# Opening token mixing with tokens standing and 512 columns of queries, keys and values moving, in a TensorE-bound two-layer trunk

## The chip, the cores and the metric

One core of one Trainium2 chip runs the whole program in one launch. The metric is device microseconds of one execution, from start to end; the time given for a kernel is the median of several runs. The engines in this text are TensorE (PE in the profile, PEld for its weight loads), VectorE (DVE), ScalarE (ACT), GpSimd (POOL) and SyncE (SP), which here only issues DMAs.

## The reference

Two layers (DEPTH 2) work on one sequence of 512 tokens by 1024 channels, in fp32. Each layer is a half-weighted SwiGLU block, a mixing block, and a second SwiGLU block:

```python
x = x + 0.5 * swiglu(rms_norm(x, ffn1_norm[l]), ffn1_wg[l], ffn1_wu[l], ffn1_wd[l])
h = rms_norm(x, mix_norm[l])
z = h @ w_in[l]                    # 1024 -> 2304 columns
q = z[..., :512]                   # 8 query heads of 64
k = z[..., 512:640]                # 2 key heads of 64
v = z[..., 640:768]                # 2 value heads of 64
attn_out = sliding_window_attention(q, k, v, attn_sink[l])
conv_out = short_conv(z[..., 768:1280], z[..., 1280:1792], z[..., 1792:], conv_w[l])
x = x + concatenate([attn_out, conv_out], -1) @ w_out[l]
x = x + 0.5 * swiglu(rms_norm(x, ffn2_norm[l]), ffn2_wg[l], ffn2_wu[l], ffn2_wd[l])
```

A last `rms_norm` follows the second layer. Attention works in blocks of 128 queries, each against its own and the previous block of 128 keys, with a bias that falls with the distance and a learned sink in the softmax. Four query heads share one key head.

## The kernel before

**Products.** TensorE's products need more precision than one fp32r product has, so each operand is split into a rounded part (hi) and the remainder (lo), and each product is three: hi x hi, hi x lo, lo x hi. ACT makes a weight's hi (line 222), DVE its lo (line 223). Raw weights come as tiles of 512 KB from HBM, most of them on SP's queue, in the order that `plan` writes down; `order` is the list of operand tiles, `need_split(g)` makes hi and lo up to tile g and issues the raw loads of some tiles further ahead (LOAD_AHEAD 4), `take_split` hands out the next tile. There are eight raw buffers and four each for hi and lo. The large products (SwiGLU, w_out) use a seven-product scheme of 2 x 2 blocks (class `Seven`), which needs sums of operand blocks.

**What stands and what moves.** A TensorE matmul has a 128 x 128 operand standing and another one moving past it. `group` (line 304) lets a tile of 128 weight columns stand and all 512 tokens move: 8 channel blocks x 3 = 24 matmuls give z for 128 columns, turned, with columns on the partitions and tokens along the row. `plain_halves`, which opens each SwiGLU block (from line 1097 on, its matmuls are the rows "up"), does it the other way: 128 tokens stand and 512 weight columns move; four weight tiles of 256 channels x 512 columns are held, and the products are done for the first 256 tokens, then for the second 256. Its result has tokens on the partitions. It is turned into columns on the partitions by a DMA: DVE and ACT write the fp32 numbers as two planes of 16 bits into a "room" (`apart`), two transposing DMAs on SP's queue turn each plane (`send`), and ACT joins the planes again (`join`).

**The norm and the opening of mixing.** The norm ahead of mixing is made in two halves of 256 tokens, because the second half's input is finished later. For each half, ACT sums squares (`Norm.__call__`), ACT makes a first guess of the reciprocal root (line 650), DVE mends it with one Newton step and scales the tokens to `xn` (line 661); `pull` then has TensorE turn xn (line 685), ACT copy hi and DVE the remainder. While the first half's turned norm is there and the second's is not, TensorE must have something to do: that is `halves` (lines 339 to 362). It holds three weight tiles (keys, values, first queries: MIX_COLS starts 2, 0 with two tiles of 128 columns each), and does for each the 24 products with 256 tokens moving, first for the first token half and then for the second; the second half's turns stand in between.

The results are `kacc`, `vacc` and `qacc`, each with its 128 columns on the partitions and 512 tokens along the row. Keys are copied straight from PSUM into kh and kl, each head at both partition halves (lines 1500 to 1506). Values are needed with tokens on the partitions: `take_values` copies vacc to SBUF and has TensorE turn it four times (line 1513). In the loop of lines 1663 to 1676 the first queries come from qacc and the other three from `group`; ACT writes hi scaled by 1/8 and DVE lo.

**Attention.** A unit is one block of 128 queries with one key head and its four query heads. `attend(step)` starts those stages of units that are due at that step by the lists at lines 44 to 49. `scores` does eight matmuls, DVE adds the bias and finds the maximum, ACT makes the exponentials (line 1565), DVE scales them by the sum (line 1573). `turn` has TensorE turn the probabilities (rows "pt", line 1623); for units whose entry in SEND_AT is a number it is done by 16-bit planes and transposing DMAs instead. `values` does the product with the values. The first scores stand at step 5, the first `turn` at step 6; step j + 2 follows the queries j, and the steps after that stand one behind each of the twelve products of the convolution's columns.

**Order.** The order on each engine is that of the program text, as far as a planner decides that an instruction is not ready; `issue_after` and `behind` pin an instruction behind another one, and `by_hand` to `by_itself` fix TensorE's order to the written one around the opening.

**Copies of the second SwiGLU block's norm.** Behind mixing stands another norm. Its `turn` also keeps a full-precision copy (`keep`, on ACT), which is put on the list `later` (lines 707 and 710) to be issued behind an instruction named by a string: "squared" is the last sum of squares on ACT, "added" a DVE addition of the block sums, "guess" the first guess of the root on ACT.

Of the kernel before, what the change touches and what calls it, by code (L numbers as in the profile page):

```python
# [8 lines left out]
F32 = mybir.dt.float32  # L9
# [7 lines left out]
P = 128  # L17
D = 1024
S = 512
# [57 lines left out]
def trunk_kernel(  # L77
# [32 lines left out]
    def psum(tag, shape, name):  # L110
        return ps.tile(shape, F32, tag=tag, bufs={"mm": 4, "sc": 2, "aux": 2}[tag], name=name)
# [215 lines left out]
    def by_itself():  # L327
        state["region"].__exit__(None, None, None)

    def hold(norm, n):  # L330

        first = state["group"]
        if norm.added:
            for ahead, one in ((2, norm.added), (3, norm.first)):
                with behind(one):
                    need_split(first + ahead)
        return [take_split(SPLIT_AHEAD - j)[1:] for j in range(n)]

    def halves(norm, n, done):

        first = state["group"]
        held = hold(norm, n)
        accs = [psum("mm", [P, S], f"acc_{first + j}") for j in range(n)]
        for t in range(2):
            for half in range(2):
                for j, (hi, lo) in enumerate(held):
                    for k in range(KC // 2 * half, KC // 2 * (half + 1)):
                        xh, xl = norm.half(k, t)
                        for i, (w, x_) in enumerate(((hi, xh), (hi, xl), (lo, xh))):
                            nc.tensor.matmul(  # L350
                                accs[j][:, t * H : (t + 1) * H],
                                w[:, k, :],
                                x_,
                                start=t + k + i == 0,
                                stop=k == KC - 1 and i == 2,
                                skip_group_check=True,
                            )
                    if not t and half and j < 2:
                        norm.pull()
                    if t and half:  # L360
                        need_split(first + j + SPLIT_AHEAD + 1)
                        done(j, accs[j])

    def down(acts, blocks, open_):

# [81 lines left out]
    def plan():  # L447
# [66 lines left out]
    MIX_COLS = (2, 0, 1, 5, 7, 3, 6, 8, 4)  # L514
    plan()


# [64 lines left out]
    class Norm:  # L582
# [39 lines left out]

        def __call__(self, t, o):

            self.squared = nc.scalar.activation(
                junk(f"sq_{self.i}_{t}_{o}"),
                xt(t, o),
                AF.Square,
                accum_out=self.ss[:, o * NT + t : o * NT + t + 1],
            )  # L630
# [48 lines left out]
        def turn(self, t, o, xn):  # L679

            name = f"{self.i}_{t}_{o}"
            tok = slice(t * P, (t + 1) * P)
            tp = psum(self.tags.pop(0), [P, KC // 2, P], f"xt_{name}")
            for j in range(KC // 2):
                nc.tensor.transpose(tp[:, j, :], xn[:, j * P : (j + 1) * P], ident)
# [12 lines left out]

            def keep():
                if not self.mixing:  # L700
                    nc.scalar.copy(self.full[o][:, :, tok], tp)

            if self.later is None:
                rest()
                keep()
            elif o:
                self.later.extend(((rest, "added"), (keep, "squared")))
            else:
                rest()
                self.later.append((keep, "squared"))  # L710

        def go_on(self):

# [293 lines left out]
    def ffn(norm, stages, whole, after=None, late=None):  # L1007
# [41 lines left out]
        def plain_halves(b):  # L1049
# [37 lines left out]
            for half in range(2):  # L1087
# [2 lines left out]
                ups = g2(f"up_{name}_{half}", F32, (P, 2, H))  # L1090
                for j, (wh, wl) in enumerate(held):
                    for t in range(2):
                        tok = slice(t * P, (t + 1) * P)
                        for k in range(2):
                            xh, xl = norm.half(2 * j + k, half)
                            for i, (x_, w) in enumerate(((xh, wh), (xl, wh), (xh, wl))):
                                nc.tensor.matmul(  # L1097
                                    accs[t],
                                    x_[:, tok],
                                    w[:, k, :],  # L1100
                                    start=j + k + i == 0,
                                    stop=j == 3 and k == 1 and i == 2,
                                )
                        if j == 3:
                            nc.scalar.activation(ups[:, t, :], accs[t][:, :H], AF.Silu)
                            nc.vector.tensor_mul(ups[:, t, :], accs[t][:, H:], ups[:, t, :])
# [380 lines left out]
    def mix(l, norm, after):  # L1487
# [8 lines left out]
        kacc, vacc, qacc = opened  # L1496
# [3 lines left out]
        for g in range(NKV):  # L1500
            own = slice(g * HD, (g + 1) * HD)
            other = slice((1 - g) * HD, (2 - g) * HD)
            nc.scalar.copy(kh[g][own, :], kacc[own, :])
            nc.vector.tensor_sub(kl[g][own, :], kacc[own, :], f32(kh[g][own, :]))
            nc.scalar.copy(kh[g][other, :], f32(kh[g][own, :]))
            nc.scalar.copy(kl[g][other, :], f32(kl[g][own, :]))

        def take_values():
            vf = g2(f"vf_{l}")
            nc.scalar.copy(vf, vacc)  # L1510
            vp = psum("aux", [P, NT, NKV, HD], f"vp_{l}")
            for t in range(NT):
                nc.tensor.transpose(
                    vp[:, t].rearrange("p g d -> p (g d)"), vf[:, t * P : (t + 1) * P], ident
                )


            vv = g8(f"vv_{l}", F32R, (P, NT * NKV, 2, HD))
            vsrc = vp.rearrange("p t g d -> p (t g) d")
            nc.scalar.copy(vv[:, :, 0, :], vsrc)  # L1520
            nc.vector.tensor_sub(vv[:, :, 1, :], vsrc, f32(vv[:, :, 0, :]))
            return vv

        class Unit:

# [134 lines left out]
                        done = getattr(unit, stages.get(at, "join"))() or done  # L1660
            return done

        for j in range(NH // 2):
            acc = group(norm.h) if j else qacc
            if j == 3:
                vv = take_values()
            if j % 2 == 0:
                room = both(f"q_{l}_{j}", shape=(P, 2, 2, S))
            qe, qo = room[j % 2][:, 0, :], room[j % 2][:, 1, :]
            for z, a, b in ((qe, slice(0, HD), slice(HD, P)), (qo, slice(HD, P), slice(0, HD))):  # L1670
                nc.scalar.activation(z[a, :], acc[a, :], AF.Copy, scale=1.0 / 8.0)
                nc.vector.scalar_tensor_tensor(
                    z[b, :], acc[a, :], 1.0 / 8.0, f32(z[a, :]), op0=ALU.mult, op1=ALU.subtract
                )
            q[2 * j], q[2 * j + 1] = qe, qo
            attend(2 + j)


        step = 6

# [87 lines left out]
```

## Time and profile before

| | |
|---|---|
| median of three runs | 1642.06 us (1641.43 to 1642.24) |
| the profiled execution | 1641.66 us, of which the span of the page is 1639.9 us |
| mean granted TensorE clock | 0.999 of full speed |
| instructions | 21080 |
| HBM read, written | 263.74 MB, 2.10 MB (162 GB/s over the span) |
| moved by hardware queue q1, by software queue q0 | 227.99 MB, 78.65 MB |
| chain that ended last, by engine | PE 92%, DVE 4%, ACT 1%, DMA 1% |

The profile is one execution. A busy time is the time in which an engine had at least one instruction under way; matmuls overlap each other, and their weight loads (PEld) run beside them. A row of the timeline reads: start in us from the start of the span, length in us, engine, line of the kernel, instruction, output <- inputs, tile shape, count; in brackets stands the idle time of the engine ahead of it and who ended that. In the lists of groups, the two numbers behind the bar are the busy time in us of all and the mean ns of one, then the idle time ahead of them. In the view of waits, a row says which engine's group waited, for whom, and then the total in us, how often, and the longest wait.

### The profile page before, as it was taken

What the parts mean: (1) busy time and instruction counts of PE and PEld (TensorE: products, weight loads), DVE (VectorE), ACT (ScalarE), POOL (GpSimd) and SP (SyncE); (2) the same over time, 40 slices, a digit from 0 to 9 for tenths busy, and PEclk for the clock granted to TensorE, in tenths of its full rate; (3) what the DMA queues carried; (4) which work ended last, traced back from release to release, by engine and by line L of the source; (5) the groups of instructions that cost most, each with busy time, mean ns of one, the idle gap of its engine ahead of it and who ended that gap; (6) DMA issues with size and microseconds to landing.
All of it is one profiled execution on the core that took longest, in us unless ns stands there. A gap on an engine that the chain in (4) does not pass through costs nothing.

```text
span 1639.9 us, 21080 instructions
## 1 busy us (share of the span) xinstructions
PE 1629.8 (99%) x7576; PEld 1356.7 (83%) x7576; DVE 1300.8 (79%) x1718; ACT 1128.7 (69%) x1581; POOL 193.5 (12%) x172
## 2 busy tenths in 40 slices
PE   9999999999999999999999999999999999999998
PEld 7888888888888888888888888888988888888886
DVE  7987779877799867798788677896578987768895
ACT  7457777556867667786576777865587775777864
POOL 0011111100111111112001111110002101111111
PEclk9999999999999999999999999999999999999999
DMA  9379999932685788999837898996137857999991
GB/s 257 86 196 219 225 215 256 221 93 58 167 205 129 205 205 206 218 228 248 231 78 204 207 218 220 232 250 194 53 90 167 208 131 191 213 224 223 227 263 65
DMA packets 286844, 308.64 MB, mean 188 GB/s; under 512 B 108532, under 2 KB 171028, under 8 KB 286740
## 3 DMA queue, kind: packets, MB, share of 16 engines
q1 hardware_dynamic: 244212, 227.99, 47.8%
q0 software_dynamic: 41824, 78.65, 28.1%
q8 instruction: 59, 0.97, 0.2%
q10 hardware_dynamic: 704, 0.66, 0.1%
q14 instruction: 45, 0.37, 0.1%
HBM read 263.74 MB, written 2.10 MB: 162 GB/s over the span
## 4 chain that ended last, share of the span: by engine, by line
PE 92%; DVE 4%; ACT 1%; DMA 1%; issue 1%; SPq 0%; ACTq 0%; DVEq 0%
PE x L941 25%; PE y L941 13%; PE x_s L941 10%; PE w L941 6%; PE y_s L941 5%; PE down L373 3%; PE acc L314 3%; PE acc L315 3%; PE acc L317 3%; PE up L1097 3%; PE w_s L941 3%; PE acc L350 2%; DVE wl L223 1%; PE acc L839 1%; DMA raw<-in_w_out_dram 1%
## 5 line engine op out<-in xcount | busy, mean ns | idle before, releaser
L223 DVE TENSOR_TENSOR wl<-raw,wh 128x1024 fp32r<-128x1024 f32 (+1 forms) x493 | 596.2, 1214 | 219.9 <-ACT wh L222 216.7
L222 ACT CAST wh<-raw 128x1024 fp32r<-128x1024 f32 (+1 forms) x493 | 513.2, 1046 | 312.2 <-PE y L941 41.6
L941 PE MATMUL y<-wh,ft 128*128 128x512 f32 x608 | 187.3, 389 | 0.0
L941 PE MATMUL x<-wh,fb 128*128 128x512 f32 x608 | 187.3, 389 | 0.0
L941 PE MATMUL x<-wh,ft 128*128 128x512 f32 x608 | 187.3, 389 | 0.0
L941 PEld LDWEIGHTS x<-wh,ft 128*128 128x128 f32 x608 | 114.1, 188 | 23.7
L941 PEld LDWEIGHTS x<-wh,fb 128*128 128x128 f32 x608 | 114.1, 188 | 23.7
L941 PEld LDWEIGHTS y<-wh,ft 128*128 128x128 f32 x608 | 114.1, 188 | 23.7
L941 PE MATMUL y<-wl,ft 128*128 128x512 f32 x304 | 118.3, 389 | 0.0
L941 PE MATMUL x<-wl,fb 128*128 128x512 f32 x304 | 118.3, 389 | 0.0
L941 PE MATMUL x<-wl,ft 128*128 128x512 f32 x304 | 118.3, 389 | 0.0
L217 POOL DMA_DIRECT2D raw<-in_ffn_wu_dram x39 | 47.3, 1222 | 544.3 <-DMA raw<-in_ffn_wu_dram 327.0
L1266 ACT COPY raw_a<-pt 128x1024 uint16<-128x1024 uint16 x76 | 103.2, 1358 | 11.1 <-DMA pt<-pl 11.1
L314 PE MATMUL acc<-hh,wh 128*128 128x512 f32 x240 | 94.7, 394 | 0.0
L315 PE MATMUL acc<-hl,wh 128*128 128x512 f32 x240 | 93.8, 391 | 0.0
L317 PE MATMUL acc<-hh,wl 128*128 128x512 f32 x240 | 93.7, 391 | 0.0
L941 PE MATMUL w<-wh,fb 128*128 128x512 f32 x304 | 93.6, 389 | 0.0
L941 PE MATMUL x_s<-wh,ft_s 128*128 128x512 f32 x256 | 78.8, 389 | 0.0
L941 PE MATMUL y_s<-wh,ft_s 128*128 128x512 f32 x256 | 78.8, 389 | 0.0
L250 DVE TENSOR_TENSOR raw<-raw,raw 128x1024 f32<-128x1024 f32 x58 | 70.6, 1222 | 7.1 <-DMA raw<-in_ffn_wd_dram 5.9
L217 POOL DMA_DIRECT2D raw<-in_ffn_wg_dram x39 | 47.1, 1212 | 233.7 <-DVE u L1250 62.3
L941 PE MATMUL x_s<-wh,fb_s 128*128 128x512 f32 x240 | 73.9, 389 | 0.0
(364 smaller groups left out, 3421.3 us busy)
## 6 DMA issues: line engine op xcount, KB each, us to landing
raw<-in_ffn_wu_dram SPq DMA_DIRECT2D x120, 512.0 KB, 5.2
raw<-in_ffn_wd_dram SPq DMA_DIRECT2D x104, 512.0 KB, 6.3
raw<-in_ffn_wg_dram SPq DMA_DIRECT2D x80, 512.0 KB, 4.9
raw<-in_ffn_wu_dram POOLq DMA_DIRECT2D x39, 512.0 KB, 8.1
raw<-in_ffn_wg_dram POOLq DMA_DIRECT2D x39, 512.0 KB, 6.0
raw<-in_w_in_dram SPq DMA_DIRECT2D x36, 512.0 KB, 4.3
raw<-in_ffn_wd_dram POOLq DMA_DIRECT2D x32, 512.0 KB, 8.5
raw<-raw POOLq DMA_DIRECT2D x20, 512.0 KB, 8.5
```

The costliest lines, as they stand in the source:

```text
L217: nc.gpsimd.dma_start(out=r, in_=rows_of(*more), accum_op=ALU.add)
L222: cast = nc.scalar.copy(hi, raw)
L223: state["sub"] = eng.tensor_sub(lo, raw, f32(hi))
L250: nc.vector.tensor_add(a11, a11, s1)
L314: nc.tensor.matmul(acc, hi[:, k, :], rhs[k][0], start=k == first, stop=False)
L315: nc.tensor.matmul(acc, hi[:, k, :], rhs[k][1], start=False, stop=False)
L317: nc.tensor.matmul(acc, lo[:, k, :], rhs[k][0], start=False, stop=k == last)
L350: nc.tensor.matmul(accs[j][:, t * H : (t + 1) * H], w[:, k, :], x_, start=t + k + i == 0, stop=k == KC - 1 and i == 2, skip_group_check=True,)
L373: nc.tensor.matmul(acc, a[:, k, tok], w[:, k, :], start=i + k + n == 0 and fresh[t], stop=i == last and k == 1 and n == 2, skip_group_chec ...
L941: nc.tensor.matmul(accs[u], x_[:, 2 * h + k, tok], w[:, k, :], start=start and h + k + i == 0, stop=h + k == 2 and i == 2, skip_group_chec ...
L1097: nc.tensor.matmul(accs[t], x_[:, tok], w[:, k, :], start=j + k + i == 0, stop=j == 3 and k == 1 and i == 2,)
L1266: nc.scalar.copy(room.rearrange("p c (n z) -> p c z n", z=2)[:, :, z, :], turned[0][:, NT * z + 2 * c : NT * z + 2 * c + 2, :],)
```

## The change

There are two independent parts.

**The opening of mixing.** `halves` is gone. The first 512 columns that mixing takes (MIX_FIRST = 0 and 2: queries 0 to 3, then keys and values, in groups of 256) are loaded as four tiles of 256 channels x 512 columns, each by two DMAs, and multiplied with tokens standing, by `standing`, which is cut out of `plain_halves` and shared with it. The bank of each 128 tokens then has 256 columns of queries, 128 of keys and 128 of values. `lay` copies the first 384 columns to SBUF, makes the values' hi and lo straight from the bank, and writes the 384 columns' 16-bit planes into a room. `send` turns them by two DMAs for each token half. `join_half` joins the planes and makes kh, kl and the first two pairs of queries for a half of the tokens: the first half's ahead of the third query group, the second half's behind the fourth. The values' turns on TensorE are gone. The scores' and turns' steps keep their numbers; only two query groups are left ahead of step 5.

**The copies kept behind the norm.** In `turn`, `keep` is issued behind "guess" and no longer behind "squared".

```diff
+    def standing(acc, norm, j, half, t, wh, wl):
+        tok = slice(t * P, (t + 1) * P)
+        for k in range(2):
+            xh, xl = norm.half(2 * j + k, half)
+            for i, (x_, w) in enumerate(((xh, wh), (xl, wh), (xh, wl))):
+                nc.tensor.matmul(
+                    acc, x_[:, tok], w[:, k, :],
+                    start=j + k + i == 0, stop=j == 3 and k == 1 and i == 2,
+                )
-    def halves(norm, n, done):
...
             ffn(ffn1_wg[l], ffn1_wu[l], ffn1_wd[l], INNER if l else FIRST)
+            for k in range(0, KC, 2):
+                u = add_unit(*((w_in[l], k, 2, 2 * c * P, 2 * P) for c in MIX_FIRST))
+                beside.add(u)
+                order.append((u, None))
...
-    MIX_COLS = (2, 0, 1, 5, 7, 3, 6, 8, 4)
+    MIX_FIRST = (0, 2)
+    MIX_COLS = (1, 5, 7, 3, 6, 8, 4)
...
-                self.later.extend(((rest, "added"), (keep, "squared")))
+                self.later.extend(((rest, "added"), (keep, "guess")))
...
-                self.later.append((keep, "squared"))
+                self.later.append((keep, "guess"))
...
-        opened = []
-        halves(norm, 3, lambda j, acc: opened.append(acc))
+        first = state["group"]
+        held = hold(norm, 4)
+        kq = 3 * P
+        vv = g8(f"vv_{l}", F32R, (P, NT * NKV, 2, HD))
...
+        def lay(half, t, acc):
+            flat = g2(f"kq_{l}_{t}", F32, (P, kq))
+            nc.scalar.copy(flat, acc[:, :kq])
+            own = slice(NKV * t, NKV * (t + 1))
+            new = acc[:, kq:].rearrange("p (g d) -> p g d", g=NKV)
+            nc.scalar.copy(vv[:, own, 0, :], new)
+            nc.vector.tensor_sub(vv[:, own, 1, :], new, f32(vv[:, own, 0, :]))
+            src = flat.bitcast(U16).rearrange("p (n z) -> p z n", z=2)
+            at = t % 2 * kq
+            with tc.issue_after(state["cast"].ins):
+                for z in range(2):
+                    nc.scalar.copy(rooms[half][:, z, at : at + kq], src[:, z])
+
+        def send(half, seen):
+            for z in range(2):
+                with tc.issue_after(seen.ins):
+                    nc.sync.dma_start_transpose(
+                        rooms[half][:, 2 + z].rearrange("p (g q) -> p g q", q=P),
+                        rooms[half][:, z],
+                    )
+
+        for half in range(2):
+            seen = state["load"]
...
+            for j, (wh, wl) in enumerate(held):
+                for t in range(2):
+                    standing(accs[t], norm, j, half, t, wh, wl)
+                    if j == 3:
+                        lay(half, 2 * half + t, accs[t])
+                if not half and j in (1, 2):
+                    norm.pull()
+                if half:
+                    need_split(first + 4 + j)
+            send(half, seen)
...
-        def take_values():
...
+        def split_q(j, src, tok):
...
+                last = nc.scalar.activation(z[a, tok], src[a, tok], AF.Copy, scale=1.0 / 8.0)
...
+        def join_half(half, *also):
+            tok = slice(half * H, (half + 1) * H)
+            with behind(state["cast"], state["sub"], *also):
+                for c in (2, 0, 1):
...
+                    dst = own[:, tok].bitcast(U16).rearrange("p (t q z) -> p z t q", q=P, z=2)
+                    for z in range(2):
+                        turned = rooms[half][:, 2 + z].rearrange("p (t c q) -> p c t q", c=3, q=P)
+                        nc.scalar.copy(dst[:, z], turned[:, c])
+                    if c < 2:
+                        split_q(c, own, tok)
+                        continue
+                    for g in range(NKV):
+                        here = slice(g * HD, (g + 1) * HD)
+                        other = slice((1 - g) * HD, (2 - g) * HD)
+                        nc.scalar.copy(kh[g][here, tok], own[here, tok])
+                        nc.vector.tensor_sub(kl[g][here, tok], own[here, tok], f32(kh[g][here, tok]))
+                        nc.scalar.copy(kh[g][other, tok], f32(kh[g][here, tok]))
+                        nc.scalar.copy(kl[g][other, tok], f32(kl[g][here, tok]))
...
-        for j in range(NH // 2):
-            acc = group(norm.h) if j else qacc
-            if j == 3:
-                vv = take_values()
...
+        join_half(0)
+        for j in (2, 3):
+            last = split_q(j, group(norm.h), slice(0, S))
             attend(2 + j)
+        join_half(1, last)
```

More of the change, by code (lines that the diff above doesn't have):

```diff
@@ L328, in by_itself @@
         state["region"].__exit__(None, None, None)
+    def standing(acc, norm, j, half, t, wh, wl):
[4 more added lines that the diff above has]
+                nc.tensor.matmul(
+                    acc,
+                    x_[:, tok],
+                    w[:, k, :],
+                    start=j + k + i == 0,
+                    stop=j == 3 and k == 1 and i == 2,
+                )
     def hold(norm, n):
@@ L337, in hold @@
         return [take_split(SPLIT_AHEAD - j)[1:] for j in range(n)]
-    def halves(norm, n, done):
[L341 to L362, printed above, removed]
     def down(acts, blocks, open_):
@@ L623, in __call__ @@
         def __call__(self, t, o):
[L625 removed]
+            nc.scalar.activation(
                 junk(f"sq_{self.i}_{t}_{o}"),
@@ L1092, in plain_halves @@
                     for t in range(2):
[L1093 to L1103, printed above, removed]
+                        standing(accs[t], norm, j, half, t, wh, wl)
                         if j == 3:
@@ new lines, in send @@
+        def send(half, seen):
[7 more added lines that the diff above has]
+            seen = state["load"]
+            rooms.append(
+                xpool.tile([P, 4, 2 * kq], U16, tag="xf", bufs=8, name=f"kq_{l}_half{half}")
+            )
+            accs = [psum("mm", [P, S], f"kqv_{l}_{2 * half + t}") for t in range(2)]
+            for j, (wh, wl) in enumerate(held):
+                for t in range(2):
+                    standing(accs[t], norm, j, half, t, wh, wl)
+                    if j == 3:
[5 more added lines that the diff above has]
+            send(half, seen)
@@ L1508, in take_values @@
-        def take_values():
[L1509 to L1514, printed above, removed]
-                )
[L1518 to L1522, printed above, removed]
+        def split_q(j, src, tok):
+            if j % 2 == 0 and tok.start == 0:
+                room_of[j // 2] = both(f"q_{l}_{j}", shape=(P, 2, 2, S))
+            qe, qo = (room_of[j // 2][j % 2][:, i, :] for i in range(2))
+            for z, a, b in ((qe, slice(0, HD), slice(HD, P)), (qo, slice(HD, P), slice(0, HD))):
+                last = nc.scalar.activation(z[a, tok], src[a, tok], AF.Copy, scale=1.0 / 8.0)
+                nc.vector.scalar_tensor_tensor(
+                    z[b, tok], src[a, tok], 1.0 / 8.0, f32(z[a, tok]), op0=ALU.mult, op1=ALU.subtract
+                )
+            q[2 * j], q[2 * j + 1] = qe, qo
+            return last
@@ new lines, in join_half @@
+        def join_half(half, *also):
+            tok = slice(half * H, (half + 1) * H)
+            with behind(state["cast"], state["sub"], *also):
+                for c in (2, 0, 1):
+                    if not half:
+                        joined.append(g2(f"kq_{l}_joined{c}"))
+                    own = joined[(2, 0, 1).index(c)]
+                    dst = own[:, tok].bitcast(U16).rearrange("p (t q z) -> p z t q", q=P, z=2)
[12 more added lines that the diff above has]
+                        nc.scalar.copy(kl[g][other, tok], f32(kl[g][here, tok]))
```

20 lines of the change are left out of this document (3 added, 17 removed).

## The prediction

> **What bounds the kernel now.** I read the page first, then who waited for whom on TensorE (PE), then the chain of waits and the timelines around the start of mixing. This is part 1 of the page:
>
> ```profile
> PE 1629.8 (99%) x7576; PEld 1356.7 (83%) x7576; DVE 1300.8 (79%) x1718; ACT 1128.7 (69%) x1581; POOL 193.5 (12%) x172
> ```
>
> TensorE has work in 1629.8 of the span's 1639.9 us, so an edit pays only if it shortens TensorE's own stream or one of its few stalls, and costs only if it makes a new one. These are the stalls, from the view of waits:
>
> ```profile
> PE xt L685 <- DVE xn L661: 0.8, 2, 0.4
> PE acc L350 <- DVE wl L223: 0.5, 1, 0.5
> PE y_m L941 <- ACT wh L222: 0.3, 1, 0.3
> ```
>
> L350 is the opening of mixing that the change replaces. Two rows of the chain of waits give the pace of the two kinds of matmul:
>
> ```profile
> 348.85 10.07 PE acc L350 x84
> 510.58 13.62 PE up L1097 x60
> ```
>
> 84 matmuls with 256 columns moving take 10.07 us, 0.1199 us each; 60 with 512 columns (tokens standing, the code that the change reuses) take 13.62 us, 0.2270 us each. Two narrow ones cost 0.2398 us, 12.8 ns more than a wide one.
>
> **The change part by part. Term 1, the products.** Per layer 144 narrow matmuls (keys, values, first queries) and 24 wide ones (second queries) become 96 wide ones. So 72 pairs are replaced by 72 wide matmuls: 72 x 0.0128 = 0.92 us a layer, 1.84 us for two. The kind is in the trace, so this is known to about 0.1 us.
>
> [...]
>
> **Term 2, the values' transposes and a late weight.** The timeline on TensorE, layer 0:
>
> ```profile
> 341.98 0.28 PE L350 MATMUL acc<-hl,wh 128*128 128x256 f32 x1
> 342.78 0.39 PE L350 MATMUL acc<-hh,wl 128*128 128x256 f32 x1 [0.52 <-DVE wl L223]
> 343.00 0.28 PE L350 MATMUL acc<-hh,wh 128*128 128x256 f32 x1
> ...
> 375.11 0.60 PE L1513 MATMUL vp<-ident,vf 128*128 128x128 f32 x4
> 375.46 0.30 PE L1544 MATMUL sc<-k,q 128*128 128x128 f32 x1
> 376.39 0.44 PE L314 MATMUL acc<-hh,wh 128*128 128x512 f32 x1
> 381.93 0.28 PE L1544 MATMUL sc<-k,q 128*128 128x256 f32 x1
> 382.05 0.28 PE L1545 MATMUL sc<-k,q 128*128 128x256 f32 x1
> 383.35 0.33 PE L1623 MATMUL pt<-ident,p 128*128 128x128 f32 x1
> ```
>
> The four value transposes hold TensorE from 375.11 to 375.46: 0.35 us a layer, 0.70 in all, gone because the values now come out with tokens on the partitions. The narrow opening needed its third weight tile after 24 matmuls x 0.12 us; from 341.98 to 342.78 it waited 0.80 us where 0.12 is normal, and the next step was 0.22: 0.78 us, in layer 0 alone.
>
> Three more rows, the first matmul of the opening, the late remainder, and the second half's norm:
>
> ```profile
> 338.99 0.28 PE L350 MATMUL acc<-hh,wh 128*128 128x256 f32 x1
> 341.51 1.22 DVE L223 TENSOR_TENSOR wl<-raw,wh 128x1024 fp32r<-128x1024 f32 x1
> 343.30 2.74 DVE L661 SCALAR_TENSOR_TENSOR xn<-x,y,gain 128x512 f32<-128x512 f32 x4
> ```
>
> With wide matmuls the third tile is due after 24 x 0.2270 = 5.4 us, at 338.99 + 5.4 = 344.4, and the second row has it done at 341.51 + 1.22 = 342.73. The wait goes and nothing takes its place: the transposes of the second token half are due then too, and their first operand is done a quarter of 2.74 us after 343.30, at 343.99.
>
> Gains together: 1.84 + 0.70 + 0.78 = 3.3 us.
>
> **Term 3, what ScalarE must do before the first probabilities turn.** Before, q1, q2 and q3 (three groups of 24 wide matmuls) stand between the opening and the first scores; after, only q2 and q3. And ScalarE (ACT) gets the packing, the joining and the splitting of turned keys and queries. Built, the ACT queue holds, from the last standing product (call its end E) to the first probabilities: one token tile's lay (a 384-wide copy, a 128-wide one, two 384-wide 16-bit packs), 3 weight casts, 9 joins of 256, 7 key copies of 256, 4 query activations of 256, 4 of 512 (q2, q3), the Exp table, and the exponentials of unit 0. Prices, from groups of ACT instructions by form:
>
> ```profile
> L222 ACT CAST wh<-raw 128x1024 fp32r<-128x1024 f32 x486 | 509.5, 1053 | 310.7 <-PE y L941 41.6 <-PE acc L315 31.6 <-issue 30.2
> L1608 ACT COPY p<-pr 128x1024 uint16<-128x1024 uint16 x12 | 15.7, 1359 | 0.0
> L1588 ACT COPY pr<-p 128x1024 uint16<-128x1024 uint16 x12 | 12.0, 1045 | 0.0
> L1671 ACT ACTIVATE q<-acc 64x512 fp32r<-64x512 f32 x16 | 9.5, 594 | 7.7 <-DVE q L1672 7.5
> L1076 ACT COPY act<-pr 128x512 uint16<-128x512 uint16 x12 | 8.4, 772 | 0.0
> L1062 ACT COPY pr<-up 128x512 uint16<-128x512 uint16 x12 | 6.9, 619 | 4.0 <-DVE up L1106 4.0
> L1565 ACT ACT_TABLE_LOAD x2 | 2.6, 1283 | 0.0
> L1505 ACT CAST k<-k 64x512 fp32r<-64x512 f32 x4 | 2.5, 621 | 0.1
> L1503 ACT CAST k<-acc 64x512 fp32r<-64x512 f32 x4 | 2.3, 580 | 0.0
> ```
>
> The 256- and 384-wide forms are not in the trace; I take the straight line through the two widths that are. Joins: (1359-772)/512 x 256 below 772 = 0.48 us. Packs: 0.51. Copies fall by (1053-621)/512 = 0.84 ns an element: 0.41 for 256, 0.47 and 0.26 for the lay's two; query activations 0.40. Then these rows of ACT's and VectorE's (DVE) timeline:
>
> ```profile
> 372.70 0.59 ACT L1671 ACTIVATE q<-acc 64x512 fp32r<-64x512 f32 x1 [1.39 <-DVE q L1672]
> 380.43 0.41 ACT L1565 ACTIVATE p<-p,nm 128x128 f32<-128x128 f32 x1 [0.32 <-DVE nm L1559]
> 381.99 0.20 ACT L1568 ACTIVATE es<-es 128x4 f32<-128x4 f32 x1
> 383.01 0.87 DVE L1573 TENSOR_SCALAR p<-p,sums 128x128 f32<-128x128 f32 x4
> 391.17 2.00 ACT L1588 COPY pr<-p 128x1024 uint16<-128x1024 uint16 x2
> ```
>
> Exponentials 380.43 to 382.19 = 1.76; from there to the transpose at 383.35 is 1.16, less 0.4 for a score reduction that is not in between afterwards: 0.75. Each q pair is 0.59 + wait + 0.59; the wait is 1.39 in the row and 7.5/8 = 0.94 on average. Sum with 1.39: lay 1.75, casts 3.16, joins 4.32, keys 2.87, narrow queries 1.60, pairs 5.14, table 1.28, exponentials 1.76, DVE 0.75: 22.6 us. With the average wait it is 0.9 less. Two copies that don't wait for each other take 2.00 instead of 2.09, so they overlap by 0.09; some 25 of the 32 instructions do: 2.4 less. I take 19.2 us, plus 0.4 until ACT sees E.
>
> TensorE reaches the first probabilities' transpose, which now stands after six of the next eight scores, after 48 x 0.2270 = 10.9 (q2, q3), 376.39-375.46 = 0.93 (scores), 381.93-376.39 = 5.54 (a product), 6 x 0.12 = 0.7: 18.1 us. So it stalls 0.4 + 19.2 - 18.1 = 1.5 us, in each layer: 3.0 us. In the trace before, that transpose (383.35) starts right behind the probability written from 383.01 on, so there is no reserve. Bounds: no overlap and full waits 4.9 us a layer; pairs that never wait (22.6 - 2.8) and the overlap (2.4) give 17.4 and no stall. What comes late next is nothing else: everything downstream on TensorE moves with it.
>
> **Term 4, the copies behind the guess.** In both mixes the last norm's copies hf now issue after the guess of the root. The timeline before, DVE and ACT:
>
> ```profile
> 502.87 0.16 DVE L649 TENSOR_TENSOR v<-ss 128x2 f32<-128x2 f32 x1
> 502.94 1.23 DVE L223 TENSOR_TENSOR wl<-raw,wh 128x1024 fp32r<-128x1024 f32 x1
> 503.60 0.30 ACT L650 ACTIVATE r<-v,eps 128x2 f32<-128x2 f32 x1
> 504.07 0.17 DVE L653 TENSOR_SCALAR v<-v 128x2 f32<-128x2 f32 x1
> 505.64 1.29 PE L685 MATMUL xt<-ident,xn 128*128 128x128 f32 x8 [0.42 <-DVE xn L661]
> ```
>
> The guess can start near 503.1 instead of 503.60, but the next step of the root (504.07, on DVE) stands behind the weight remainder that ends at 502.94 + 1.23 = 504.17, the same instant within the view's rounding, and that order is the same after the change. So the stall at 505.64 stays: 0. Bounds: nothing to the whole 0.8 us that the view of waits gives for both layers.
>
> **Term 5, what else moves.** Four transposing DMAs a layer join SP's queue among the w_in loads; each waits for ACT's packs, and the loads behind it wait too.
>
> ```profile
> raw<-in_w_in_dram SPq DMA_DIRECT2D x36, 512.0 KB, 4.3
> pr<-pr SPq DMA_TRANSPOSE x18, 3.2
> ```
>
> The first half's transposes have the whole second half (48 x 0.2270 = 10.9 us) before ACT reads them and need 3.2; the second half's are read behind q3. Loads run four groups (21.8 us) ahead and need 4.3. Cost 0; without that cover a late tile would cost what exceeds it.
>
> Sum: -3.3 + 3.0 = -0.3 us on the profiled execution (1641.66 us, of which 1639.9 span), and so on the median 1642.06, which stands 0.4 above it: 1641.7 us. A measurement of this kernel can tell about 0.2% (3.3 us) from no change.
>
> **Rivals.** A, slower: ACT's queue is the new bound. Its place is the first transpose of probabilities; it decides from an ACT list over 17.7 us and costs two us for each us above. At the bound of 22.6 it gives -3.3 + 9.8 = +6.5: 1648.6. For it: no reserve before, and 32 small instructions in a row; against it: independent ones overlap in the trace. [...] B, faster: the list fits in 17.7 us; the full gain stays, 1638.7, and if the guess also frees the stall of term 4, 1637.9. For it: part of the list (casts, second q pair) may slip into DVE's waits; against: ACT waits nowhere else in it. [...] That the change doesn't do what it says holds for its last part: the guess moves and nothing follows, which is in the sum.
>
> **How the numbers follow.** Forecast 0.52, A 0.24, B 0.19, C 0.05. Half of the forms in the ACT list are untried at these widths, and both ends of it are within two tenths of its length, so A and B keep much. A passes +3.3 us from a list of 21.0 on, which most of its cases reach: slower 0.22. B lies at the bound itself and beyond it with a little of term 4: faster 0.19. Same takes the rest, 0.59. The range leaves out A's cases with a list over 21.5 (-3.3 + 2 x 3.8 = +4.3) and B's with more than half a us of term 4: 1638.2 to 1646.3.
>
> **What would show it.** L350's rows gone and 192 wide ones at 0.227 us in their place; no L1513; no wait for wl near 342; a new wait of TensorE on the first pt of each layer of 1 to 2 us, with ACT busy without a break from E on; the waits on xn near 505 and 1315 unchanged. It is wrong if TensorE waits at scores, at kqv or on a w_in weight, or if the joins take much more or less than 0.48 us.

## The result, and the profile after

| | before | after |
|---|---|---|
| median of nine runs | 1641.71 us (1640.78 to 1642.48) | 1646.53 us (1645.54 to 1648.96) |
| profiled execution, span | 1641.66, 1639.9 us | 1647.38, 1645.6 us |

The ratio is 1.0031 (95% interval 1.0021 to 1.0041): the changed kernel is 4.8 us slower. Busy times per engine, from the page of the changed kernel:

```profile
PE 1628.5 (99%) x7424; PEld 1348.9 (82%) x7424; DVE 1304.6 (79%) x1736; ACT 1149.1 (70%) x1653; POOL 193.6 (12%) x172
```

TensorE has 152 matmuls fewer and is busy 1.3 us less, yet the span is 5.7 us longer. ScalarE has 72 instructions and 20.4 us more. The waits of TensorE, changed kernel (total, how often, longest):

```profile
PE pt L1662 <- DVE p L1612: 5.7, 3, 2.5
...
PE x_s L935 <- DVE wl L223: 0.8, 2, 0.4
PE xt L679 <- DVE xn L655: 0.8, 2, 0.4
```

The wait for a late weight in the opening is gone, the waits for xn are as before, and the transposes of the first probabilities wait, 2.5 us in each layer; a third wait of that row (0.7) stands at unit 2's transposes in layer 1. Where the 5.7 us lie is seen by stretches. First from the opening's first matmul to the first scores, before and after (start and end, then length, busy time of TensorE and its matmuls, granted clock, DMA share, GB/s):

```profile
338.99:375.46 36.47, 35.95 (x237) 1.00 0.27 80
1149.55:1185.25 35.70, 35.70 (x238) 1.00 0.20 59
```

```profile
339.09:373.57 34.48, 34.48 (x161) 1.00 0.40 106
1152.91:1187.34 34.43, 34.43 (x162) 1.00 0.33 84
```

Up to here the change gains 36.47 - 34.48 = 1.99 us in layer 0 and 35.70 - 34.43 = 1.27 in layer 1. Then from the opening to the first turns of the next norm, again before and after:

```profile
338.99:493.76 154.77, 153.92 (x800) 1.00 0.53 131
1149.55:1303.27 153.72, 153.67 (x800) 1.00 0.52 127
```

```profile
339.09:495.67 156.58, 153.85 (x723) 0.99 0.55 134
1152.91:1308.98 156.07, 152.73 (x723) 1.00 0.53 130
```

Over the whole of mixing layer 0 loses 156.58 - 154.77 = 1.81 us and layer 1 156.07 - 153.72 = 2.35. So what follows the first scores costs 3.8 and 3.6 us. Outside mixing, only the stretch from the end of the first of these to the start of the second differs by much, 657.24 against 655.79 us, 1.45 more. It holds two short waits at x_s (a product of the seven-product scheme; the third in the view stands in layer 0), 1.1 us together by the spacing of the matmuls, in the second layer's first SwiGLU block. In the profiled executions of the first two runs below, whose code there is the same, the view has no wait at x_s. That stretch took 655.7 to 655.8 us in four of the nine later executions with the wide opening and 656.4 to 658.1 in the other five, so it varies with the execution. Both executions with the narrow opening had 655.8; whether the wide opening makes these waits likelier stays open.

What follows the first scores, on TensorE in layer 0, from the last score ahead of the transposes:

```profile
380.56 0.28 PE L1584 MATMUL sc<-k,q 128*128 128x256 f32 x1
383.33 0.47 PE L1662 MATMUL pt<-ident,p 128*128 128x128 f32 x1 [2.50 <-DVE p L1612]
...
385.53 0.63 PE L317 MATMUL acc<-hh,wl 128*128 128x512 f32 x1
385.95 0.63 PE L314 MATMUL acc<-hh,wh 128*128 128x512 f32 x1
386.38 0.43 PE L315 MATMUL acc<-hl,wh 128*128 128x512 f32 x1
386.65 0.40 PE L317 MATMUL acc<-hh,wl 128*128 128x512 f32 x1
386.89 0.39 PE L314 MATMUL acc<-hh,wh 128*128 128x512 f32 x1
```

The transposes could have started at 380.68 and start at 383.33: 2.65 us. And behind the wait the products start up to 0.43 us apart (385.53, 385.95, 386.38) in place of 0.227, until 386.4. The granted clock in that stretch (same columns as above):

```profile
382.00:383.00 1.00, 0.00 (x0) 1.00 0.00 0
383.50:386.00 2.50, 2.50 (x10) 0.50 0.01 2
386.50:387.00 0.50, 0.50 (x4) 1.00 1.04 293
```

In stretches of 0.1 us the clock is halved from 383.04, still within the wait, to 386.45. From the first transpose to the seventh product behind it TensorE took 3.56 us (383.33 to 386.89); in layer 1, where the same wait left the clock at 1.00, the same instructions took 2.17 us (1197.10 to 1199.27). So the halved clock cost 1.4 us beyond the wait. In layer 1 the transposes of unit 2 waited instead, 1213.42 being 0.86 us after the last matmul's normal step:

```profile
1197.10 0.33 PE L1662 MATMUL pt<-ident,p 128*128 128x128 f32 x1 [2.50 <-DVE p L1612]
...
1212.34 0.39 PE L317 MATMUL acc<-hh,wl 128*128 128x512 f32 x1
1213.42 1.25 PE L1662 MATMUL pt<-ident,p 128*128 128x128 f32 x8 [0.70 <-DVE p L1612]
```

Sum for layer 0: -2.0 + 2.65 + 1.4 = +2.0 (measured 1.81); for layer 1: -1.27 + 2.65 + 0.86 = +2.2 (measured 2.35).

What VectorE's p waits for is ScalarE. Its timeline in layer 0, from the last token tile's packing to the exponentials' end, shows it at work throughout but for two waits of 1.53 and 0.75:

```profile
362.89 0.49 ACT L1488 COPY kq<-kqv 128x384 f32<-128x384 f32 x1
...
365.21 1.18 ACT L1551 COPY kq_joined<-kq_half 128x256 uint16<-128x256 uint16 x3
366.23 0.84 ACT L1558 CAST k<-kq_joined 64x256 fp32r<-64x256 f32 x2
...
374.40 0.59 ACT L1533 ACTIVATE q<-acc 64x512 fp32r<-64x512 f32 x1 [1.53 <-DVE q L1534]
...
377.44 0.59 ACT L1533 ACTIVATE q<-acc 64x512 fp32r<-64x512 f32 x1 [0.75 <-DVE q L1534]
378.06 1.16 ACT L1551 COPY kq_joined<-kq_half 128x256 uint16<-128x256 uint16 x3
379.10 0.40 ACT L1558 CAST k<-kq_joined 64x256 fp32r<-64x256 f32 x1
379.51 1.28 ACT L1604 ACT_TABLE_LOAD   x1
...
382.36 0.19 ACT L1607 ACTIVATE es<-es 128x4 f32<-128x4 f32 x1
```

From 362.89 to the transposes at 383.33 the list takes 20.44 us. The two waits in it, 2.28 us, are for VectorE's remainders of the queries; no run below shortens them alone.

### The profile page after: what moved, and what is told of

It is laid out like the page before. It is cut to its first block, busy times and chain, and to the rows that moved or that the text cites. A ratio compares the mean times of both kernels' runs of the same rounds, so it can differ in the third digit from the quotient of the medians.

```text
span 1645.6 us, 20902 instructions
## 1 busy us (share of the span) xinstructions
PE 1628.5 (99%) x7424; PEld 1348.9 (82%) x7424; DVE 1304.6 (79%) x1736; ACT 1149.1 (70%) x1653; POOL 193.6 (12%) x172
## 4 chain that ended last, share of the span: by engine, by line
PE 87%; DVE 6%; ACT 4%; DMA 2%; issue 1%; SPq 0%; DVEq 0%; ACTq 0%; POOLq 0%
PE x L935 25%; PE y L935 13%; PE x_s L935 9%; PE w L935 6%; PE y_s L935 5%; PE down L362 3%; PE up L336 3%; PE acc L314 3%; PE acc L315 3%; PE kqv L336 2%; PE acc L317 2%; PE w_s L935 2%; DVE wl L223 2%; DMA raw<-in_ffn_wd_dram 1%; PE acc L833 1%
## 5 line engine op out<-in xcount | busy, mean ns | idle before, releaser
L314 PE MATMUL acc<-hh,wh 128*128 128x512 f32 x224 | 89.1, 398 | 0.0
L315 PE MATMUL acc<-hl,wh 128*128 128x512 f32 x224 | 87.6, 391 | 0.0
L317 PE MATMUL acc<-hh,wl 128*128 128x512 f32 x224 | 87.6, 391 | 0.0
```

Of the source, the lines that this page charges most:

```text
L314: nc.tensor.matmul(acc, hi[:, k, :], rhs[k][0], start=k == first, stop=False)
L315: nc.tensor.matmul(acc, hi[:, k, :], rhs[k][1], start=False, stop=False)
L317: nc.tensor.matmul(acc, lo[:, k, :], rhs[k][0], start=False, stop=k == last)
```

## The experiments

The theory to begin with: ScalarE's list ends 2.65 us after TensorE is ready for the first transposes, and that wait also trips the clock. Rival 1 has the clock's dip as incidental, rival 2 seeks the loss outside mixing. Each run below has five rounds against the kernel before on the same chip.

### Four runs on the wait and the clock

**The control.** In step 6, all scores stand ahead of the transposes:

```diff
+            if step == 6 and SCORES_AT in what:
+                what = (VALUES_AT, JOIN_AT, SCORES_AT, TURN_AT, SEND_AT)
```

> The changed kernel with one reordering: at step 6 the eight scores of unit 1 all stand ahead of unit 0's probability transposes (six of them did). It is the control of the next run. Theory (the ScalarE list ends late and TensorE waits for it; the wait also halves TensorE's clock for a few us in most executions): the wait at the first transposes is 2.2 to 2.5 us a layer, the mean granted clock 0.997 to 0.998, the time within 0.8 us of the changed kernel's 1646.5. Rival 1 (the wait costs its own length and the clock's dips are incidental): the same. Rival 2 (the loss stems from waits for weights in the first SwiGLU blocks, 0.4 to 1.5 us, and not from mixing): the same here.

Measured: 1646.12 us (ratio 1.0027, 1.0017 to 1.0038), the waits 2.2 us in each layer. As expected. Here the clock fell in both layers of the profiled execution, in layer 0 from 384.69 on, 1.4 us after the wait had ended; the rows of layer 0, eight products 0.427 us apart, end like this:

```profile
387.33 0.63 PE L314 MATMUL acc<-hh,wh 128*128 128x512 f32 x1
387.76 0.56 PE L315 MATMUL acc<-hl,wh 128*128 128x512 f32 x1
388.15 0.40 PE L317 MATMUL acc<-hh,wl 128*128 128x512 f32 x1
```

Eight times 0.200 us more is 1.6 us for one fall of the clock.

**The wait filled with matmuls of zeros.**

```diff
                     tp = psum("aux", [P, 4, P], f"pt_{self.name}_{kb}")
+                    if n_of(self) == 0:
+                        spin(10, tp.rearrange("p h q -> p (h q)"))
```

> The reordered kernel with ten extra matmuls of zeros per layer, 512 columns wide, written into the bank of unit 0's transposed probabilities ahead of the transposes, so that TensorE is at work for about 2.2 us of its wait; nothing else is changed and the transposes can start no earlier. Theory: the clock stays at 0.999 in every execution, the rows behind the transposes keep 0.227 us, and the time falls by what the halved clock cost, 1.5 us an event in one or two layers: 1.5 to 3.0 us under the control. Rival 1: within 0.5 us of the control. Rival 2: within 0.5 us of the control.

Measured: 1653.68 us (1.0069, 1.0055 to 1.0083), 7.6 us over the control. Neither number came, and the mean clock was 0.995 to 0.998, at 0.999 in none of the five executions. Only behind the filled wait itself does the clock stay at 1.00, in both layers of the profiled execution. This is the table of stretches, from 380 in layer 0 and from 1194 in layer 1:

```profile
380.00:384.00 4.00, 3.96 (x21) 2.25 (x21) 1.82 (x8) 3.90 (x15) 0.00 (x0) 1.00 0.00 0
...
1194.00:1198.00 4.00, 3.96 (x23) 2.32 (x21) 1.29 (x7) 3.93 (x14) 0.00 (x0) 1.00 0.00 0
```

(busy times of PE, PEld, DVE, ACT and POOL, then the clock.) But the order changed with the extra matmuls: the planner put unit 2's transposes ahead of eight scores and six products, 2.3 us of work that had covered them, and there TensorE now waits instead:

```profile
399.01 1.34 PE L1664 MATMUL pt<-ident,p 128*128 128x128 f32 x8 [2.95 <-DVE p L1612]
```

Behind this new wait of 2.95 us the clock falls in layer 1 and not in layer 0. So the run doesn't price the clock, and two filled waits are too few to show that idleness trips it: in layer 1 of the changed kernel an unfilled one left the clock alone. What all the traces say of this stands in the last section. The run does show something else: the next transposes are just as short of time as the first.

**The second half's joins behind the exponentials.**

```diff
-                nc.scalar.activation(es, es, AF.Exp)
+                self.exps = nc.scalar.activation(es, es, AF.Exp)
...
-        join_half(1, last)
+        join_half(1, last, todo[0].exps)
```

> The changed kernel with the second half's joins and splits pinned behind unit 0's last exponential; the work is the same. In the changed kernel's trace three joins and a key copy (378.06 to 379.51) stand ahead of the Exp table. Theory: the exponentials start 1.45 us sooner, the wait at the first transposes falls from 2.5 to about 1.05 us a layer, which no longer halves the clock: 2.9 us less for the waits and up to 3 us less for the clock, 1640.6 to 1643.6. Rival 1: 2.9 us less and no more, 1643.6. Rival 2: no change, 1646.5 within 1 us.

Measured: 1643.39 us (1.0011, 1.0002 to 1.0020): 3.1 us off. The waits are 1.3 us in each layer, the clock 0.999 in nine of eleven runs. The waits fell, to 1.3 and not to 1.05 us. The time lies within the theory's range and 0.2 us from rival 1's number, so it doesn't decide between them; TensorE now also waits 0.8 us in four places for VectorE ahead of products with the values.

**The first transposes one step later.**

```diff
-TURN_AT = (6, None, 8, None, 11, None, 14, 15)
+TURN_AT = (7, None, 8, None, 11, None, 14, 15)
...
-VALUES_AT = (7, 11, 9, 13, 12, 15, 15, 16)
+VALUES_AT = (8, 11, 9, 13, 12, 15, 15, 16)
```

> The changed kernel with unit 0's transposes one step later (step 7 in place of 6) and its values at step 8 in place of 7, so that a further product of 5.45 us stands ahead of them. Theory: no wait at the first transposes, clock 0.999, the whole gain of the wide opening is left: 3.3 us under the kernel before, 1638.4 within 1 us, unless a later transpose waits in its place. Rival 1: the same. Rival 2: at least 1641.7, since the waits outside mixing stay.

Measured: 1648.09 us (1.0030, 1.0019 to 1.0041), no better than the change itself. The theory as I had it, one late point that needs 2.65 us, falls here. From TensorE's timeline in layer 0:

```profile
386.89 0.60 PE L1662 MATMUL pt<-ident,p 128*128 128x128 f32 x4
...
388.80 0.39 PE L1583 MATMUL sc<-k,q 128*128 128x256 f32 x1 [0.70 <-DVE q L1534]
...
400.34 1.03 PE L1662 MATMUL pt<-ident,p 128*128 128x128 f32 x4 [2.11 <-DVE p L1612]
```

The first transposes wait for nothing, and the same time is lost behind them, 0.70 at the scores of unit 2 and 2.11 at its transposes. Unit 2's probabilities were scaled, counted from the opening's first matmul in layer 0, at 58.1 us before, and at 60.5, 60.7, 60.0, 59.5 and 60.3 in the changed kernel and these four runs. Where TensorE stands when it waits hardly matters to that time. This suggests that ScalarE's list as a whole is too long up to that point, and that a later date for one item moves the wait to the next. If so, what helps must take work off ScalarE, which the next runs try.

### Four runs on ScalarE's list

**The key copies on VectorE**, which in the changed kernel is busy for 7.5 of the 12 us from 374 to 386, and for 6.1 of the 12 us ahead of them:

```diff
-                        nc.scalar.copy(kh[g][other, tok], f32(kh[g][here, tok]))
-                        nc.scalar.copy(kl[g][other, tok], f32(kl[g][here, tok]))
+                        nc.vector.tensor_copy(kh[g][other, tok], f32(kh[g][here, tok]))
+                        nc.vector.tensor_copy(kl[g][other, tok], f32(kl[g][here, tok]))
```

> The changed kernel with the copies of the keys' hi and lo to the other half of the partitions (eight of 64 x 256 a layer, 0.40 to 0.41 us each on ScalarE, four of them ahead of the first exponentials) done by VectorE. Theory (ScalarE's list as a whole is too long as far as unit 2's probabilities, ready 60.0 to 60.7 us after the opening in all four variants so far against 58.1 before): the first wait falls from 2.5 by 4 x 0.41 = 1.6 to 0.9 us a layer, unit 2's probabilities are ready by 58 to 59, the clock stays at 0.999; time 1640.5 to 1643. Rival (VectorE's remainders of keys and queries are what the scores and probabilities wait for): VectorE has 8 copies more, the waits stay or grow, 1646 or more.

Measured: 1640.88 us (0.9998, 0.9989 to 1.0007), 5.6 us under the changed kernel's median. (The late joins had 59.5, so the four variants lie at 59.5 to 60.7.) The first waits are 1.3 us, where 0.9 was expected; unit 2's probabilities are scaled at 58.4 us, and its transposes don't wait. The rival falls. VectorE does a copy in 0.28 us where ScalarE took 0.40:

```profile
L1560 DVE CAST k<-k 64x256 fp32r<-64x256 f32 x8 | 2.3, 289 | 0.2
L1561 DVE CAST k<-k 64x256 fp32r<-64x256 f32 x8 | 2.3, 282 | 0.0
```

**Both**, these copies and the late joins:

> The copies on VectorE, and the second half's joins behind unit 0's last exponential. Theory: 1.6 and 1.45 us off the 2.5 us of the first wait leave none, and unit 2's do not wait either: the wide opening's whole gain is left, 3.3 us under the kernel before, 1638.4 to 1639.5. Rival: as above, 1643 or more.

Measured: 1638.72 us, 0.9981 of the kernel before (0.9972 to 0.9990), as the theory has it. No transposes wait any more, and the two layers' mixing takes the same time to the hundredth, with TensorE busy all through it:

```profile
338.76:491.10 152.34, 152.29 (x723) 1.00 0.57 139
1149.19:1301.53 152.34, 152.25 (x724) 1.00 0.55 133
```

Against the kernel before that is 2.43 and 1.38 us less.

**The second part of the change undone**, copies behind "squared" again:

```diff
-                self.later.extend(((rest, "added"), (keep, "guess")))
+                self.later.extend(((rest, "added"), (keep, "squared")))
...
-                self.later.append((keep, "guess"))
+                self.later.append((keep, "squared"))
```

> The changed kernel with its second part undone: the norm's kept copies issue behind the last sum of squares again. Theory: this part is worth nothing either way, since the root's next step waits on VectorE; 1646.5 within 1 us, and TensorE's waits on xn stay 0.4 us each. Rival: the part costs or brings up to 0.8 us.

Measured: 1647.01 us (1.0029, 1.0019 to 1.0039), the waits for xn still 0.4 us each. The part does nothing that can be measured.

**The joins on VectorE too**, beside the copies and the late order (`nc.vector.tensor_copy(dst[:, z], turned[:, c])`):

> The copies and the joins (12 of 128 x 256, 16 bits, a layer, 0.35 us each on ScalarE) on VectorE, and the second half behind unit 0's last exponential. Theory: ScalarE is freed of a further 4.2 us a layer; with no wait left after the run before it brings nothing more, 1638.4 to 1639.5. Rival (VectorE is then the later of the two): a wait of TensorE for VectorE's key or query remainders, 1640 or more.

Measured: 1640.23 us (0.9990, 0.9982 to 0.9999). The rival's number came, though at another place than it named: the transposes wait 0.8 us again. The joins are cheaper on VectorE, 0.31 us in place of 0.48, but VectorE then has the maxima of unit 0 ready 1.0 us later (39.3 in place of 38.2 us after the opening). Its interval overlaps that of the run with both, so that it is worse is likely, not shown; in its one trace mixing takes 1.4 us more.

### Two controls

**The key copies on VectorE in the kernel before**, where the lines are those at 1505 and 1506:

> The kernel before, with its eight copies of the keys to the other half of the partitions (64 x 512, 0.62 us each on ScalarE) done by VectorE; the opening stays narrow. It asks whether the 3.1 us of the copies on VectorE with the late joins come from the wide opening or from the copies alone. Theory (from the wide opening, once ScalarE keeps up; before the change nothing waited for ScalarE there): within 1 us of the kernel before, 1641.7. Rival (freeing ScalarE pays in either kernel): 1639 or less.

Measured: 1642.00 us (1.0002, 0.9993 to 1.0011). Freeing ScalarE alone brings nothing: the 3.1 us come from the wide opening, once ScalarE keeps up with it.

**The key copies on GpSimd**, with the late joins (`nc.gpsimd.tensor_copy` in the place of `nc.vector.tensor_copy`):

> The changed kernel with the second half's joins behind unit 0's last exponential and the key copies on GpSimd in place of VectorE. GpSimd has nothing else in that stretch. Theory (it only matters that ScalarE is rid of them, as long as the keys come before unit 1's scores): 1638.4 to 1640, as with VectorE. Rival (GpSimd takes 1 us or more for each copy, which no row shows, and the scores of unit 0 or 1 wait for the keys): 1641 or more, with TensorE waiting at a score.

Measured: 1639.40 us (0.9986, 0.9977 to 0.9994); GpSimd takes 0.52 and 0.44 us a copy, and no score waits. It does as well as VectorE within the intervals.

The wait, the clock and the time in all these runs. The clock is the mean granted clock that each execution gave (for the kernel before, in those beside the runs above); mixing is the sum of both layers' stretches from the opening to the next norm's turns, in the profiled execution:

| kernel | TensorE's longest wait for probabilities | runs at 0.999 | mixing, us | median us |
|---|---|---|---|---|
| kernel before | none | 71 of 72 | 308.5 | 1641.71 |
| changed kernel | 2.5 us | 1 of 9 | 312.7 | 1646.53 |
| its second part undone | 2.5 | 1 of 9 | 312.2 | 1647.01 |
| scores first | 2.2 | 3 of 8 | 312.9 | 1646.12 |
| matmuls of zeros | 2.9 | 0 of 5 | 317.7 | 1653.68 |
| transposes a step later | 2.1 | 2 of 7 | 313.3 | 1648.09 |
| late joins | 1.3 | 9 of 11 | 309.1 | 1643.39 |
| key copies on VectorE | 1.3 | 9 of 11 | 306.5 | 1640.88 |
| both | none | 9 of 11 | 304.7 | 1638.72 |
| joins on VectorE too | 0.8 | 10 of 11 | 306.1 | 1640.23 |
| kernel before, key copies on VectorE | none | 10 of 11 | 308.2 | 1642.00 |
| key copies on GpSimd, late joins | none | 10 of 11 | 305.0 | 1639.40 |

Rival 2, a loss outside mixing, falls for most of the loss: 4.2 of the 5.7 us of the profiled execution lie in mixing. Waits of 2.1 us and more go with a clock under 0.999 in most runs (31 of 38), waits of 1.3 us in 4 of 22, hardly more often than none at all behind the wide opening (3 of 22). Within the kernel with the transposes a step later, the two runs at 0.999 took 1645.33 and 1645.82 us and the four at 0.997 1647.90 to 1648.44. The same split of medians gives 2.6 us there, 1.6 with the scores first, 1.3 in the changed kernel and 0.5 with its second part undone, the last two from a single run at 0.999 each. The traces show why it differs. Without waits the wide opening's mixing takes 152.34 us in either layer. In the changed kernel the layer whose clock fell took 156.58 and the other 156.07, only 0.5 us less, because there unit 2's transposes waited instead. With the transposes a step later nothing behind waits instead, and the two layers took 157.43 and 155.82, 1.6 us apart. So rival 1, by which the dips are incidental, falls too, but a fall's net price was 0.5 to 1.6 us, less than that of the late list itself.

## Why the prediction was wrong

It gave 1641.7 us within 1638.2 to 1646.3; measured were 1646.53. Step by step:

- **Term 1 and 2, right.** The sum of the two terms up to the first scores was 0.92 + 0.35 + 0.78 = 2.05 us in layer 0 and 1.27 in layer 1; the stretches gave 1.99 and 1.27. The wide matmuls of the opening run 0.227 us apart (the first 24 start from 339.09 to 344.30), which is the pace that the prediction took from the row at L1097; the narrow pairs' surplus was had back, and the wait for the late weight went with nothing in its place.
- **Term 3, right mechanism, too small: the first step that failed.** Place, engine and missing reserve were as said: 1.5 us a layer forecast, 2.65 measured. The prices of single instructions were good (a join 0.48 us forecast, 0.483 measured; a key copy 0.41 and 0.40; the packs 0.51 and 0.53). What failed is the reckoning of how they add up. The gross sum of 22.6 us came down to 20.4, and I had taken 19.2 (its own rows give 22.6 - 0.9 - 25 x 0.09 = 19.5, which would have moved the forecast by 0.6 us): I allowed the lower wait between query pairs (two of 0.94) and the overlap of 25 instructions (2.4 us) at once. Measured, the two waits sum to 2.28 where the gross sum had 2.78, and the overlap is 22.6 - 0.5 - 20.4 = 1.7 us, most of it in the joins (nine elapse 3.1 us where they sum to 4.3). With 20.4 the prediction's own formula gives 0.4 + 20.4 - 18.1 = 2.7 us a layer, the measured wait, and -3.3 + 2 x 2.65 = +2.0, which is 1643.7 on the 1641.71 of the nine runs.
- **"What comes late next is nothing else", wrong, and about as dear.** I let a wait cost its own length. It costs more in one of two ways. Either the clock halves around it, 1.4 us in layer 0 of the changed kernel; or it doesn't, and unit 2's transposes wait a further 0.86 us, as in layer 1, since ScalarE's backlog isn't worked off by then (it is busy for 14.0 of the 14.4 us from 1199.0 to 1213.4). In the profiled execution these two, 2.3 us, account for the 2.1 us by which the loss in mixing (4.2) exceeds the +2.0 above. The other 0.7 us up to the 4.8 of the medians isn't located. The run with the transposes a step later shows that the backlog comes back at the next item.
- **Term 4, right**: 0 forecast, nothing measured when it was undone.
- **Term 5, right**: no load of w_in is waited for, and the transposing DMAs land in 2.8 us (3.2 forecast):

```profile
kq_half<-kq_half SPq DMA_TRANSPOSE x8, 2.8
```

- **Rival A** is what came, in place and kind, at a time its list alone doesn't give: its formula needs a list of 21.8 us for +4.8 (17.7 + 8.1 / 2), and the list was 20.4. **Rival B**'s full gain is real (1638.7 forecast for a list that fits, 1638.72 measured with the copies on VectorE and the late joins), only not in this kernel. The agreement to the hundredth is luck: the interval is 1637.1 to 1640.1, and mixing alone gained 3.8 us where 3.3 was forecast.

## What to carry to other kernels

When work moves off a full engine onto one that is 69% busy, the share says nothing: add up the receiving engine's list between two of the full engine's needs, and on to the next need and the one after, because a late list that is given a later date is late again (here 2.50 us at the first transposes became 0.70 and 2.11 behind them). Take at most one favourable allowance in such a sum. And don't price a new stall of the matmul engine at its length alone: here 2.65 us cost 3.7 and 4.2 a layer (156.07 and 156.58 us of mixing, against 152.34 in the run without waits).

## What the runs showed of the hardware

Five of the traces have waits of 2.1 to 2.95 us on TensorE in mixing, ten in all. Around six of the ten the granted clock fell from 1.00 to 0.50; the mean clock of these five executions was 0.997 to 0.998. In the other seven traces, with a mean clock of 0.999, it fell nowhere in mixing, not around the four waits of 1.3 us either. Whether it fell differed from layer to layer of one execution, with waits equal to a hundredth (2.50 us in both layers of the changed kernel, where it fell in layer 0 alone), and no run shows why. In the changed kernel the slow stretch lasts 3.41 us, from 383.04 to 386.45, and matmuls with 512 columns start 0.427 us apart in it, in place of 0.227; the other five slow stretches last 3.4 us as well. Their start isn't tied to the wait's end: it lay between 0.5 us ahead of that (first layer, second part undone) and 1.6 us behind it (second layer, scores first). The matmuls behind the wait took 1.4 us longer for it in layer 0 of the changed kernel and 1.6 us in layer 0 with the scores first; the net price is less where something behind would have waited anyway, 0.5 us between the two layers of the changed kernel.

Small copies on ScalarE overlapped by different amounts: nine joins of 0.483 us took 0.34 us each in a row, while pairs of key casts and of query activations took 0.84 and 0.85 us for two of 0.41, no overlap at all. A single overlap read from two neighbouring copies is no price for a mixed list.
